# Six slabs kept back ahead of a Strassen pass, and operands moved from GpSimd to VectorE, in a decoder layer

## Chip, core and metric

The kernel runs on one core of a Trainium2 chip. A core has five engines that run side by side, each through its own instructions in order: TensorE (PE in the profile; its weight loads are PEld), VectorE (DVE), ScalarE (ACT), GpSimd (POOL) and SyncE (SP), which here issues most of the DMAs. PE writes its products to PSUM; DVE and ACT work on PSUM and SBUF here, POOL on SBUF. The metric is the time of one execution in microseconds (us).

## The reference, cut to what matters

One decoder layer on 512 tokens of width 2048, in float32:

```
h = RMSNorm(x);  q, k, v for two groups of heads = h @ w_in
A = stick-breaking attention, 16 heads      B = sliding-window attention (128) with sinks, 16 heads
x = x + concat(RMSNorm(A), RMSNorm(B)) @ w_out          # w_out: 2048 x 2048
h = RMSNorm(x);  x = x + (silu(h @ w_gate) * (h @ w_up)) @ w_down     # 5632 wide
out = RMSNorm(x)
```

The change touches the stretch from the sliding-window attention (B) through the output projection `@ w_out` to the first operands of the gate/up product.

## The kernel before

Float32 products are made from rounded halves. Each operand is split into a high half (a copy rounded to the matmul's type, made by ACT) and a low half (the operand less its high half, made by DVE), and high x high, low x high and high x low are added up in PSUM. So each weight that arrives has to be rounded twice before PE can use it, and each left operand too.

**Slabs.** Plain projections run off one list, `queue`, of slabs: a weight tile of 256 rows x 512 columns, read by one DMA on SP's queue into one of three `raw` buffers, rounded by `split` (ACT's `whi` at L221, DVE's `wlo` at L222; two buffers each), then used in eight steps of three matmuls (L382 to L384). `step()` runs one step. At the third step of a slab the two slabs behind it are loaded and the next one is rounded. `pull(ns)` runs steps until a nominal time is used up, `drain(mark)` runs all up to a slab number. `a_end` is the number of slabs up to the end of `outA`, the product with the upper half of w_out (group A's part): four column blocks of four slabs.

**Sliding-window stage.** 18 rounds of a software pipeline over 16 jobs (scores, exponentials, transposes at L1146, products with V at L1159 and L1160), between which `pull(SWFILL / 4, a_end - 3)` runs slabs four times a round. The last job of each head group sums squares of its output into `sqB` (squares by ACT at L729, sums by POOL at L730) and scales the output `oB` by the norm's gain. Behind the rounds three slabs of `outA` are left.

**Strassen pass for group B.** The product of `oB` with the left half of the columns in the lower half of w_out (`OutPass`) is a Strassen-like scheme: seven products in 14 slots (0 to 13), each with weights that are sums or differences of blocks (`sum`, by POOL, from blocks loaded by `load`) and left operands that are sums or differences of blocks of `oB` (`add`) which are rounded (`form`: ACT's high half, then a low half). Plain left operands are rounded by `split_b` into `mhi` and `mlo`. Weights here have their low half taken against a second rounded copy, `hp`, in PSUM. What happens ahead of the pass is a plan by slot numbers: slots -6 to -1, each `b_slot(n)` (loads, sums, roundings of weights for slots n + 1 and n + 2), four steps of the three slabs, then the slot's "late" entries. At slot -4 `sumsq_rstd` turns `sqB` into the norm's factor `rstdB`: matmuls with ones (L735), a copy out of PSUM (L738), a variance `rv` (L278), logarithm and exponential on ACT (L280, L282), and four small DVE operations (L284 to L288).

**Order.** Instructions called through `pV`, `pA`, `pG`, `pT` and `dma` (all at L118 or L100 in the profile) stay in program order on their engine; others may be moved by the scheduler at build time when it thinks an engine free.

**Operands of gate/up.** Behind the pass the right half of the columns follows as eight plain slabs (`add_outB`). Over their steps `h2_split` turns finished columns of x into `xh`, and `form(p, 0, parts)` makes the left operands of another Strassen scheme for the first half of the rows: "+" a sum or difference in place, "h" the high half by ACT, "l" the low half. `form(p, 1, ...)` does so for the second half later.

Of the kernel before, what the change touches and what calls it, by code (L numbers as in the profile page):

```python
# [8 lines left out]
F32 = mybir.dt.float32  # L9
# [3 lines left out]
AF = mybir.ActivationFunctionType  # L13
ALU = mybir.AluOpType
AX = mybir.AxisListType

P = 128
S = 512
NT = S // P
# [3 lines left out]
SBW = 1024  # L23
# [4 lines left out]
EPS = 1e-5  # L28
# [9 lines left out]
def tile_hymba(ctx: ExitStack, tc: tile.TileContext, x, ln_mix, w_in, sb_norm, swa_norm,  # L38
# [6 lines left out]
    const = ctx.enter_context(tc.tile_pool(name="const", bufs=1))  # L45
    sm = ctx.enter_context(tc.tile_pool(name="sm", bufs=4))
# [10 lines left out]
    def open_z(name):  # L57

        if zs[0] is not None:
            zs[0].close()  # L60
        zs[0] = ExitStack()
        zs[1] = zs[0].enter_context(tc.tile_pool(name=name, bufs=1, space=bass.MemoryType.PSUM, reuse_waits="tile"))
# [12 lines left out]
    def pz():  # L75
        return zs[1].tile([P, 512], F32, tag="z", name="z", bufs=4)

    def po():
        return bank("o", 2)
# [22 lines left out]
    def f(ap):  # L102
        return ap.bitcast(F32)

    mm = nc.tensor.matmul
    V = nc.vector
    A = nc.scalar
    G = nc.gpsimd
# [11 lines left out]
    pV, pA, pG, pT = Pinned(V), Pinned(A), Pinned(G), Pinned(nc.tensor)  # L120
# [5 lines left out]
    ones = const.tile([P, P], F32, name="ones")  # L126
# [129 lines left out]
    def pull(ns, mark=None):  # L256

        mark = len(queue) if mark is None else mark
        carry[0] += ns
        while carry[0] > 0 and pos[0] < mark:  # L260
            carry[0] -= step()
# [4 lines left out]
    def drain(mark=None):  # L266

        mark = len(queue) if mark is None else mark
        while pos[0] < mark:
            step()  # L270
# [273 lines left out]
    def at_slot(n, stage, fn, *args):  # L544
        plan.setdefault((n, stage), []).append((fn, args))

    def run(n, stage):
        for fn, args in plan.pop((n, stage), ()):
            fn(*args)
# [182 lines left out]
    def sumsq_rstd(acc, name, pb=None):  # L732
        pb = po() if pb is None else pb
        for t in range(NT):
            mm(pb[:, 2 * t:2 * t + 2], lhsT=acc[:, t * P:(t + 1) * P], rhs=ones[:, 0:2],  # L735
               start=(t == 0), stop=True, skip_group_check=True)
        sst = sm.tile([P, NT], F32, tag="sst", name="sst")
        V.tensor_copy(out=sst, in_=pb[:, 0:2 * NT].rearrange("p (t two) -> p t two", two=2)[:, :, 0])  # L738
        return rstd_from(sst, NT, 1.0 / SBW, name)
# [232 lines left out]
    def at(fn, j):  # L972
        if 0 <= j < NJ:
            fn(*jobs[j])
# [32 lines left out]
    sqB = const.tile([P, S], F32, tag="rbc2", name="sqB")  # L1007
# [73 lines left out]
    a_end = len(queue)  # L1081
# [89 lines left out]
    blks = {}  # L1171
    jobs = [(g, blk) for g in range(4) for blk in range(NT)]
    NJ = len(jobs)
    SWFILL = 5800.0
    pull(2600.0, a_end - 3)
    at(swa_scores, 0)
    stacks = {0: lambda: stack_queries(1, 0), 1: lambda: stack_queries(1, 1), 2: lambda: stack_keys(0, 1),
              5: lambda: stack_keys(1, 0), 6: lambda: stack_keys(1, 1)}
    for j in range(NJ + 2):
        at(swa_exp, j)  # L1180
        if j == 3:
            rstdA = sumsq_rstd(sqA, "rstdA")
        if j in stacks:
            stacks[j]()
        pull(SWFILL / 4, a_end - 3)
        at(swa_tr, j - 1)
        pull(SWFILL / 4, a_end - 3)
        if j == 2:
            drain(swv_end)
        if j + 1 < NJ and jobs[j + 1][1] == 0:  # L1190
            drain(smarks[jobs[j + 1][0]])
        at(swa_av, j - 2)
        pull(SWFILL / 4, a_end - 3)
        at(swa_norm, j)
        at(swa_scores, j + 1)
        pull(SWFILL / 4, a_end - 3)
    drain(a_end - 3)
    kqs.close()

    class OutPass(Block):  # L1200
# [80 lines left out]
    rstd_b = []  # L1281
    open_phase("op", 1, reuse_waits="tile")
    bp = OutPass()
# [5 lines left out]
    for k, q, i in ((-6, "22", 0), (-6, "12", 0), (-5, "11", 0), (-4, "11", 1), (-3, "12", 1), (-2, "22", 1),  # L1289
                    (0, "21", 0), (1, "21", 1)):  # L1290
        at_slot(k, "load", bp.load, q, i)
    for k, fn, *args in ((-5, bp.add, "7", pG), (-4, bp.sum, "7", 0), (-3, bp.sum, "5", 0),
                         (-2, bp.form, "7", pV), (-1, bp.sum, "6", 0), (-1, bp.add, "3", pV),
                         (0, bp.sum, "7", 1), (1, bp.sum, "5", 1), (2, bp.form, "6", pG), (3, bp.sum, "6", 1),
                         (4, bp.sum, "4", 0), (5, bp.sum, "4", 1), (6, bp.form, "5", pG), (8, bp.form, "3", pG)):
        at_slot(k, "sum", fn, *args)
    for k in range(4):
        at_slot(k - 6, "late", split_b, k // 2, k % 2 * 2)
    for k, p in ((-4, "7"), (0, "6"), (4, "5"), (7, "3")):
        at_slot(k, "late", bp.form, p)  # L1300
    at_slot(-3, "late", bp.add, "5", pV)
    at_slot(-2, "late", bp.add, "6", pV)
    for k, p in enumerate(PD):
        at_slot(2 * k + 2, "take", bp.take, p)
    for k, c, h in ((8, 1, 0), (9, 0, 2), (11, 1, 2)):
# [3 lines left out]
    def b_slot(n):  # L1309
        run(n, "load")  # L1310
        run(n, "sum")
        bof(n + 1, "to_hi")
        bof(n + 1, "to_lo")
        bof(n + 2, "to_hp")

    for n in range(-6, 0):
        if n == -4:
            rstd_b.append(sumsq_rstd(sqB, "rstdB", pz()))
        if n == -2:
            open_z("psb")  # L1320
        b_slot(n)
        for _ in range(4):
            step()
        run(n, "late")

# [9 lines left out]
    def e8(name):  # L1335
        return side.tile([P, 4, 512], F32, tag="e8", name=name, bufs=3)
# [28 lines left out]
    def form(p, s, parts="+hl"):  # L1365


        eV, eA = (pV, pA) if s and p not in "17" else (V, A)
        xa, xb = xh[2 * s], xh[2 * s + 1]
        a11, a21 = xa[:, :, 0:256], xa[:, :, 256:512]  # L1370
        if p not in "17":
            a12, a22 = xb[:, :, 0:256], xb[:, :, 256:512]
        if "+" in parts:
            if p == "7":
                src = e8("s3")[:, 0:2, :].rearrange("p u (a b) -> p (u a) b", a=2)
                V.tensor_tensor(out=src, in0=a11, in1=a21, op=ALU.subtract)
            elif p == "5":
                src = a21
                (eV if s else G).tensor_tensor(out=src, in0=a21, in1=a22, op=ALU.add)
            elif p == "6":  # L1380
                src = a11
                (eV if s else G).tensor_tensor(out=src, in0=a21, in1=a11, op=ALU.subtract)
            elif p == "3":
                src = a12
                (pG if s else G).tensor_tensor(out=src, in0=a12, in1=a11, op=ALU.subtract)
            if p not in "124":
                fsrc[p, s] = src
        if p in "124":
            fsrc[p, s] = {"1": lambda: a11, "2": lambda: a12, "4": lambda: a22}[p]()
        src = fsrc[p, s]  # L1390
        if "h" in parts:
            hc[p, s] = form_tile(p, s)
            eA.activation(out=hc[p, s][:, :, 0:256], in_=src, func=AF.Copy)
        if "l" in parts:
            hl = hc[p, s]
            (G if s == 0 and p in "243" else eV).tensor_tensor(out=hl[:, :, 256:512], in0=src, in1=f(hl)[:, :, 0:256],
                                                                op=ALU.subtract)

    def norm_sums(c, t):
        A.activation(out=junk, in_=x2[c][:, t, :], func=AF.Square, accum_out=ss2[:, t, c:c + 1])  # L1400
# [390 lines left out]
    for j in range(NFF):  # L1791
# [7 lines left out]
        late = j < NFF - 1  # L1799
# [31 lines left out]
    for g in range(5):  # L1831
        b0, l = NS + 28 * g, lefts[g]
# [205 lines left out]
```

## Time and profile before

| | us |
|---|---|
| median of 3 runs (2000.39 to 2003.95) | 2000.72 |
| the profiled execution | 2003.73 |
| its span, first to last instruction | 2002.0 |
| PE busy in the span | 1976.7 |
| DVE / ACT / POOL busy | 1511.5 / 1524.3 / 1047.0 |
| mean granted TensorE clock | 0.994 |

The stretch of the change, in the profiled execution: the sliding-window rounds run from about 424 to 580 us, the slots ahead of the pass to 607, the pass to 651, the plain slabs of group B to 707. A timeline row gives start, duration, engine, line of the kernel, operation with tiles out<-in, and in brackets how long the engine was idle before it and what released it. A window's row gives its length and the busy time of PE, PEld, DVE, ACT and POOL, the granted clock, and the share and rate of the DMAs.

### The profile page before, as it was taken

What the parts mean: (1) busy time and instruction counts of PE and PEld (TensorE: products, weight loads), DVE (VectorE), ACT (ScalarE), POOL (GpSimd) and SP (SyncE); (2) the same over time, 40 slices, a digit from 0 to 9 for tenths busy, and PEclk for the clock granted to TensorE, in tenths of its full rate; (3) what the DMA queues carried; (4) which work ended last, traced back from release to release, by engine and by line L of the source; (5) the groups of instructions that cost most, each with busy time, mean ns of one, the idle gap of its engine ahead of it and who ended that gap; (6) DMA issues with size and microseconds to landing.
All of it is one profiled execution on the core that took longest, in us unless ns stands there. A gap on an engine that the chain in (4) does not pass through costs nothing.

```text
span 2002.0 us, 29013 instructions
## 1 busy us (share of the span) xinstructions
PE 1976.7 (99%) x10180; PEld 1688.2 (84%) x10180; DVE 1511.5 (76%) x2066; ACT 1524.3 (76%) x2043; POOL 1047.0 (52%) x458
## 2 busy tenths in 40 slices
PE   9999999999999899999999999999999999999998
PEld 8888888898877788888888888888888888888886
DVE  6676888879878787777777777777777867767767
ACT  6765877868756487777777777777777788788787
POOL 2840000000033376576666657666665778878883
PEclk9999999999998999999999999999999999999999
DMA  6415354422351445445354444535444743433523
GB/s 202 146 53 145 99 136 122 116 80 74 98 188 32 148 121 142 123 115 141 98 141 108 130 124 114 142 98 141 108 129 111 274 147 127 168 126 112 178 79 116
DMA packets 290978, 252.82 MB, mean 126 GB/s; under 512 B 12560, under 2 KB 234832, under 8 KB 288400
## 3 DMA queue, kind: packets, MB, share of 16 engines
q1 hardware_dynamic: 289072, 244.11, 41.8%
q0 software_dynamic: 1376, 5.52, 0.8%
q8 instruction: 81, 1.33, 0.3%
q10 hardware_dynamic: 384, 1.34, 0.2%
q14 instruction: 65, 0.53, 0.1%
HBM read 218.40 MB, written 19.92 MB: 119 GB/s over the span
## 4 chain that ended last, share of the span: by engine, by line
PE 92%; DVE 3%; ACT 2%; issue 2%; POOL 1%; DVEq 0%; ACTq 0%; POOLq 0%
PE o L118 37%; PE m L118 31%; PE m L418 3%; PE m L419 3%; PE m L420 3%; PE z L118 1%; PE z L933 1%; PE m L382 1%; PE m L383 1%; PE m L384 1%; PE o L961 1%; PE o L383 1%; PE o L384 1%; PE o L382 1%; PE z L1146 1%
## 5 line engine op out<-in xcount | busy, mean ns | idle before, releaser
L118 DVE TENSOR_TENSOR wlo<-t,hp 128x1024 fp32r<-128x1024 f32 x253 | 308.4, 1219 | 191.2 <-PE o L118 115.5
L118 POOL TENSOR_TENSOR t<-raw,t 128x1024 f32<-128x1024 f32 x111 | 282.6, 2546 | 281.0 <-ACT hp L118 268.7
L118 ACT ACTIVATE whi<-t 128x1024 fp32r<-128x1024 f32 x253 | 268.5, 1061 | 130.0 <-PE o L118 78.3
L118 POOL TENSOR_TENSOR t<-raw,raw 128x1024 f32<-128x1024 f32 x118 | 305.9, 2596 | 29.4 <-issue 11.7
L118 PE MATMUL o<-hca,whi 128*128 128x512 f32 x880 | 307.5, 391 | 0.0
L118 DVE TENSOR_TENSOR wlo<-raw,hp 128x1024 fp32r<-128x1024 f32 x191 | 233.2, 1221 | 92.9 <-issue 51.6
L118 ACT ACTIVATE whi<-raw 128x1024 fp32r<-128x1024 f32 (+1 forms) x193 | 204.1, 1058 | 107.4 <-PE m L118 75.2
L118 ACT ACTIVATE hp<-t 128x1024 fp32r<-128x1024 f32 x253 | 255.2, 1009 | 8.0 <-POOL t L118 4.3
L118 PE MATMUL o<-hca,wlo 128*128 128x256 f32 x880 | 244.0, 280 | 0.0
L118 ACT ACTIVATE hp<-raw 128x1024 fp32r<-128x1024 f32 x195 | 196.7, 1009 | 3.1 <-DMA raw<-in_w_down_dram 1.9
L118 PEld LDWEIGHTS o<-hca,whi 128*128 128x128 f32 x880 | 164.2, 187 | 35.8
L118 PE MATMUL m<-hca,whi 128*128 128x512 f32 x528 | 186.3, 392 | 1.1 <-DVE hca L118 1.1
L118 PEld LDWEIGHTS o<-hca,wlo 128*128 128x128 f32 x880 | 165.6, 189 | 0.4
L730 POOL TENSOR_TENSOR sqA<-sqA,oc 128x512 f32<-128x512 f32 x7 | 10.1, 1437 | 273.9 <-ACT oc L729 273.9
L118 PE MATMUL m<-whi,dca 128*128 128x512 f32 x592 | 146.9, 389 | 0.0
L118 PE MATMUL o<-whi,dca 128*128 128x512 f32 x592 | 146.8, 389 | 0.0
L118 PE MATMUL m<-hca,wlo 128*128 128x256 f32 x528 | 146.3, 280 | 0.0
L118 PEld LDWEIGHTS o<-whi,dca 128*128 128x128 f32 x592 | 111.1, 188 | 23.0
L118 PEld LDWEIGHTS m<-whi,dca 128*128 128x128 f32 x592 | 111.1, 188 | 23.0
L222 DVE TENSOR_TENSOR wlo<-raw,whi 128x1024 fp32r<-128x1024 f32 x79 | 100.2, 1268 | 35.6 <-ACT whi L221 34.1
L118 PE MATMUL m<-hcs,whi 128*128 128x512 f32 x352 | 125.9, 392 | 0.0
L418 PE MATMUL m<-hhi,whi 128*128 128x512 f32 x320 | 125.8, 393 | 0.0
(391 smaller groups left out, 5204.5 us busy)
## 6 DMA issues: line engine op xcount, KB each, us to landing
raw<-in_w_gate_up_dram SPq DMA_DIRECT2D x348, 256.0 KB, 5.2
raw<-in_w_down_dram SPq DMA_DIRECT2D x68, 512.0 KB, 5.0
raw<-in_w_in_dram SPq DMA_DIRECT2D x35, 512.0 KB, 4.7
raw<-in_w_in_dram SPq DMA_DIRECT2D x66, 256.0 KB, 4.0
raw<-in_w_out_dram SPq DMA_DIRECT2D x28, 512.0 KB, 3.8
aT<-w SPq DMA_DIRECT2D x44, 256.0 KB, 3.5
xd<-aT SPq DMA_DIRECT2D x10, 1024.0 KB, 6.6
rx<-in_w_down_dram SPq DMA_DIRECT2D x20, 512.0 KB, 5.6
```

What stands on the lines that cost most here:

```text
L118: return lambda *a, **k: tc.keep_in_program_order(fn(*a, **k))
L222: V.tensor_tensor(out=lo, in0=raw, in1=f(hi), op=ALU.subtract)
L382: mm(o, lhsT=lh[:, sl], rhs=hi[:, j, :], start=first, stop=False, skip_group_check=halves)
L383: mm(o, lhsT=lh[:, sl], rhs=lo[:, j, :], start=False, stop=False, skip_group_check=halves)
L384: mm(o, lhsT=ll[:, sl], rhs=hi[:, j, :], start=False, stop=(k == nslab * a - 1), skip_group_check=halves)
L418: mm(o, lhsT=wh, rhs=xh, start=(k == 0), stop=False)
L419: mm(o, lhsT=wh, rhs=xl, start=False, stop=False)
L420: mm(o, lhsT=wl, rhs=xh, start=False, stop=(k == KT - 1))
L730: G.tensor_tensor(out=acc, in0=acc, in1=t, op=ALU.add)
L933: mm(zb[:, o:o + r.shape[1]], lhsT=lhsT, rhs=r, start=False, stop=last, skip_group_check=True)
L961: mm(H.ob[:, c0:S], lhsT=vb, rhs=r[:, o:o + S - c0], start=(k == 3 and r is B.h), stop=(k == 0 and r is B.l), skip_group_check=True)
L1146: nc.tensor.transpose(out=pb[:, hh * P:(hh + 1) * P], in_=B.s[hh // 2][:, hh % 2, j * P:(j + 1) * P], identity=ident)
```

## The change

- Six slabs of `outA` are kept for the slots ahead of the pass, not three; `SWFILL` is 5200, not 5800; the slots run from -8 to -1 with six steps each, not from -6 with four.
- The roundings by `split_b` and the difference for the seventh product move to slots -8 and -7, the sums on `oB` and the seventh product's low half to -6 and -5. POOL's weight sums and the loads keep their slots (-6 to 1).
- `sumsq_rstd` is taken apart: matmuls and variance at -8 (the variance read from PSUM, without the copy), logarithm and exponential at -6, the small operations at -5.
- For the first half of the gate/up operands, the three sums and the three low halves that POOL made are made by DVE.

```diff
-    SWFILL = 5800.0
-    pull(2600.0, a_end - 3)
+    SWFILL = 5200.0
+    pull(2600.0, a_end - 6)
...
-        pull(SWFILL / 4, a_end - 3)
+        pull(SWFILL / 4, a_end - 6)
...
-    drain(a_end - 3)
+    drain(a_end - 6)
...
-    for k, fn, *args in ((-5, bp.add, "7", pG), (-4, bp.sum, "7", 0), (-3, bp.sum, "5", 0),
-                         (-2, bp.form, "7", pV), (-1, bp.sum, "6", 0), (-1, bp.add, "3", pV),
-                         (0, bp.sum, "7", 1), (1, bp.sum, "5", 1), (2, bp.form, "6", pG), (3, bp.sum, "6", 1),
-                         (4, bp.sum, "4", 0), (5, bp.sum, "4", 1), (6, bp.form, "5", pG), (8, bp.form, "3", pG)):
+    for k, fn, *args in ((-4, bp.sum, "7", 0), (-3, bp.sum, "5", 0), (-1, bp.sum, "6", 0), (0, bp.sum, "7", 1),
+                         (1, bp.sum, "5", 1), (2, bp.form, "6", pG), (3, bp.sum, "6", 1), (4, bp.sum, "4", 0),
+                         (5, bp.sum, "4", 1), (6, bp.form, "5", pG), (8, bp.form, "3", pG)):
         at_slot(k, "sum", fn, *args)
-    for k in range(4):
-        at_slot(k - 6, "late", split_b, k // 2, k % 2 * 2)
-    for k, p in ((-4, "7"), (0, "6"), (4, "5"), (7, "3")):
-        at_slot(k, "late", bp.form, p)
-    at_slot(-3, "late", bp.add, "5", pV)
-    at_slot(-2, "late", bp.add, "6", pV)
+    rB = {}
+    def rstdb_sum():
+        pb = pz()
+        for t in range(NT):
+            mm(pb[:, 2 * t:2 * t + 2], lhsT=sqB[:, t * P:(t + 1) * P], rhs=ones[:, 0:2], ...)
+        rB["v"] = sm.tile([P, NT], F32, tag="rv", name="rv")
+        pV.tensor_scalar(out=rB["v"], in0=pb[...], scalar1=1.0 / SBW, scalar2=EPS, op0=ALU.mult, op1=ALU.add)
+    def rstdb_exp():
...
+        pA.activation(out=l, in_=rB["v"], func=AF.Ln)
...
+        pA.activation(out=rB["r"], in_=l, func=AF.Exp, scale=-0.5)
+    def rstdb_make():
...
+        pV.tensor_tensor(out=rstd_b[0], in0=r, in1=t, op=ALU.mult)
+    for k, fn, *args in ((-8, bp.add, "7", pG), (-8, rstdb_sum), (-8, split_b, 0, 0), (-8, split_b, 0, 2),
+                         (-7, split_b, 1, 0), (-7, split_b, 1, 2), (-7, bp.form, "7"), (-6, rstdb_exp),
+                         (-6, bp.add, "5", pV), (-6, bp.add, "6", pV), (-5, rstdb_make), (-5, bp.form, "7", pV),
+                         (-5, bp.add, "3", pV), (0, bp.form, "6"), (4, bp.form, "5"), (7, bp.form, "3")):
+        at_slot(k, "late", fn, *args)
...
-    for n in range(-6, 0):
-        if n == -4:
-            rstd_b.append(sumsq_rstd(sqB, "rstdB", pz()))
+    for n in range(-8, 0):
...
-        for _ in range(4):
+        for _ in range(6):
             step()
...
-                (eV if s else G).tensor_tensor(out=src, in0=a21, in1=a22, op=ALU.add)
+                eV.tensor_tensor(out=src, in0=a21, in1=a22, op=ALU.add)
...
-                (eV if s else G).tensor_tensor(out=src, in0=a21, in1=a11, op=ALU.subtract)
+                eV.tensor_tensor(out=src, in0=a21, in1=a11, op=ALU.subtract)
...
-                (pG if s else G).tensor_tensor(out=src, in0=a12, in1=a11, op=ALU.subtract)
+                (pG if s else V).tensor_tensor(out=src, in0=a12, in1=a11, op=ALU.subtract)
...
-            (G if s == 0 and p in "243" else eV).tensor_tensor(out=hl[:, :, 256:512], in0=src, in1=f(hl)[:, :, 0:256],
-                                                                op=ALU.subtract)
+            eV.tensor_tensor(out=hl[:, :, 256:512], in0=src, in1=f(hl)[:, :, 0:256], op=ALU.subtract)
```

More of the change, by code (lines that the diff above doesn't have):

```diff
@@ L1184, in tile_hymba @@
             stacks[j]()
-        pull(SWFILL / 4, a_end - 3)
+        pull(SWFILL / 4, a_end - 6)
         at(swa_tr, j - 1)
-        pull(SWFILL / 4, a_end - 3)
+        pull(SWFILL / 4, a_end - 6)
         if j == 2:
@@ L1192, in tile_hymba @@
         at(swa_av, j - 2)
-        pull(SWFILL / 4, a_end - 3)
+        pull(SWFILL / 4, a_end - 6)
         at(swa_norm, j)
         at(swa_scores, j + 1)
-        pull(SWFILL / 4, a_end - 3)
-    drain(a_end - 3)
+        pull(SWFILL / 4, a_end - 6)
+    drain(a_end - 6)
     kqs.close()
@@ L1296, in tile_hymba @@
         at_slot(k, "sum", fn, *args)
-    for k in range(4):
-        at_slot(k - 6, "late", split_b, k // 2, k % 2 * 2)
-    for k, p in ((-4, "7"), (0, "6"), (4, "5"), (7, "3")):
-        at_slot(k, "late", bp.form, p)
-    at_slot(-3, "late", bp.add, "5", pV)
-    at_slot(-2, "late", bp.add, "6", pV)
+    rB = {}
+    def rstdb_sum():
+        pb = pz()
+        for t in range(NT):
+            mm(pb[:, 2 * t:2 * t + 2], lhsT=sqB[:, t * P:(t + 1) * P], rhs=ones[:, 0:2],
+               start=(t == 0), stop=True, skip_group_check=True)
+        rB["v"] = sm.tile([P, NT], F32, tag="rv", name="rv")
+        pV.tensor_scalar(out=rB["v"], in0=pb[:, 0:2 * NT].rearrange("p (t two) -> p t two", two=2)[:, :, 0],
+                         scalar1=1.0 / SBW, scalar2=EPS, op0=ALU.mult, op1=ALU.add)
@@ new lines, in rstdb_exp @@
+    def rstdb_exp():
+        l = sm.tile([P, NT], F32, tag="rl", name="rl")
+        pA.activation(out=l, in_=rB["v"], func=AF.Ln)
+        rB["r"] = sm.tile([P, NT], F32, tag="rr", name="rr")
+        pA.activation(out=rB["r"], in_=l, func=AF.Exp, scale=-0.5)
+    def rstdb_make():
+        r, t = rB["r"], sm.tile([P, NT], F32, tag="rt", name="rt")
+        pV.tensor_tensor(out=t, in0=r, in1=r, op=ALU.mult)
+        pV.tensor_tensor(out=t, in0=t, in1=rB["v"], op=ALU.mult)
+        pV.tensor_scalar(out=t, in0=t, scalar1=-0.5, scalar2=1.5, op0=ALU.mult, op1=ALU.add)
+        rstd_b.append(const.tile([P, NT], F32, name="rstdB"))
+        pV.tensor_tensor(out=rstd_b[0], in0=r, in1=t, op=ALU.mult)
```

## The prediction

> **What bounds the kernel now.** I read the page first, then the list of what PE waited for, then the order in time around the longest of those waits, on PE, POOL and DVE in turn. Rows of a timeline are start, duration, engine, line, operation, and in brackets the idle time before it and who ended it; rows of the wait list are total us, times, longest.
>
> ```profile
> span 2002.0 us, 29013 instructions
> PE 1976.7 (99%) x10180; PEld 1688.2 (84%) x10180; DVE 1511.5 (76%) x2066; ACT 1524.3 (76%) x2043; POOL 1047.0 (52%) x458
> ```
> ```profile
> PE m L383 <- DVE wlo L222: 6.8, 2, 4.6
> PE m L118 <- DVE wlo L118: 2.9, 1, 2.9
> PE m L382 <- ACT whi L221: 2.1, 1, 2.1
> ```
>
> PE has work for 1976.7 of 2002.0 us, so an edit off PE can win 25 us at most, plus what matmuls lose on a slow clock. Of the idle time 11.8 us is in these three rows, and all three mean the low or the high half of a weight slab. They stand in two places, both of which the diff edits. The first is just ahead of the Strassen pass of the output projection:
>
> ```profile
> 579.40 0.40 PE L1160 MATMUL z<-plo,swv 128*128 128x512 f32 x1
> ...
> 593.91 0.39 PE L384 MATMUL o<-whi,mlo 128*128 128x512 f32 x1
> 596.35 0.50 PE L382 MATMUL m<-whi,mhi 128*128 128x512 f32 x1 [2.05 <-ACT whi L221]
> 599.10 0.80 PE L383 MATMUL m<-wlo,mhi 128*128 128x512 f32 x1 [2.25 <-DVE wlo L222]
> ```
> ```profile
> 611.71 2.07 PE L118 MATMUL m<-wlo,mhi 128*128 128x512 f32 x4 [2.87 <-DVE wlo L118]
> 613.58 1.91 PE L118 MATMUL m<-whi,mhi 128*128 128x512 f32 x4
> ...
> 618.35 2.01 PE L118 MATMUL o<-whi,vf 128*128 128x512 f32 x8
> ```
>
> From 613.58 on four matmuls take 1.91 us where eight take 2.01 at 618.35: behind such idle time the clock is halved for some us. What the place costs in all: the slab that ends at 593.91 + 0.23 = 594.14 is followed by one more slab and the first product, 24 matmuls each. A slab without a wait is 24 x 0.23 = 5.5 us, so the next product could start at 605.1. It starts at 618.35. **The first place costs 13.3 us**: 7.2 idle, 6.1 slow clock.
>
> Why the halves are late, from POOL and DVE in the same stretch:
>
> ```profile
> 582.12 2.66 POOL L730 TENSOR_TENSOR sqB<-sqB,oc 128x512 f32<-128x512 f32 x2 [1.48 <-ACT oc L729]
> 584.73 0.79 POOL L118 DMA_DIRECT2D x<-in_x_dram  x1
> 585.54 2.65 POOL L118 TENSOR_TENSOR t<-oB 128x1024 f32<-128x1024 f32 x1
> 588.15 3.37 POOL L118 TENSOR_TENSOR t<-raw,raw 128x1024 f32<-128x1024 f32 x1
> 591.60 3.25 POOL L118 TENSOR_TENSOR raw<-raw,rx 128x1024 f32<-128x1024 f32 x1
> 594.93 2.36 POOL L118 TENSOR_TENSOR t<-raw,raw 128x1024 f32<-128x1024 f32 x1
> 603.72 2.39 POOL L118 TENSOR_TENSOR t<-raw,raw 128x1024 f32<-128x1024 f32 x1 [6.43 <-DVE vf L118]
> ```
> ```profile
> 585.85 6.75 DVE L118 TENSOR_TENSOR mlo<-oB,mhi 128x1024 fp32r<-128x1024 f32 x2
> ...
> 592.71 2.16 DVE L278 TENSOR_SCALAR rv<-sst 128x4 f32<-128x4 f32 x1
> ...
> 597.82 1.23 DVE L222 TENSOR_TENSOR wlo<-raw,whi 128x1024 fp32r<-128x1024 f32 x1
> ...
> 603.51 1.45 DVE L1074 SCALAR_TENSOR_TENSOR x<-m,rstdA,x 128x512 f32<-128x512 f32 x2
> ```
>
> While POOL works, two roundings take 6.75 us, and a 128x4 operation takes 2.16, both ending as a POOL operation ends; with POOL idle a rounding is 1.23. The two engines alternate: one POOL operation of 2.4, one DVE operation of 1.1. The two operations at 603.51 read a PSUM bank and take 0.73 each although POOL starts at 603.72: those aren't held. The Trainium skill (SBUF — State Buffer, "Who interferes with whom") says that a VectorE instruction with two SBUF inputs and a GpSimd instruction that reads SBUF exclude each other, the later one blocking for the whole instruction. By that rule 6.75 would be one POOL operation waited for at each rounding, and the trace agrees.
>
> The second place is the first half's operands of the gate/up stage:
>
> ```profile
> 671.74 3.32 POOL L1396 TENSOR_TENSOR hca<-xh,hca 128x1024 fp32r<-128x1024 f32 x1
> ```
> ```profile
> 662.47 1.22 DVE L222 TENSOR_TENSOR wlo<-raw,whi 128x1024 fp32r<-128x1024 f32 x1
> 667.07 5.79 DVE L1396 TENSOR_TENSOR hca<-xh,hca 128x1024 fp32r<-128x1024 f32 x2 [3.38 <-ACT hca L1393]
> 672.78 3.35 DVE L222 TENSOR_TENSOR wlo<-raw,whi 128x1024 fp32r<-128x1024 f32 x1
> ```
> ```profile
> 671.20 0.39 PE L382 MATMUL m<-whi,mhi 128*128 128x512 f32 x1
> 676.19 0.80 PE L383 MATMUL m<-wlo,mhi 128*128 128x512 f32 x1 [4.60 <-DVE wlo L222]
> ...
> 682.79 0.39 PE L384 MATMUL o<-whi,mlo 128*128 128x512 f32 x1
> ```
>
> That slab runs from 671.20 to 683.02, 11.8 us in place of 5.5: **the second place costs 6.3 us**. The cause is the same: POOL and DVE exclude each other.
>
> **The change, part by part.** Everything is PE time; the matmuls are the same, only their order moves.
>
> *Filler of the sliding-window stage.* Six slabs are held back, so 15.5 us less filler for 18 rounds; SWFILL falls by 0.6 in nominal ns, 0.63 us on PE. What a round then lacks is cover for DVE:
>
> ```profile
> 449.98:513.50 63.52, 63.17 (x329) 52.59 (x327) 62.08 (x156) 51.47 (x125) 2.38 (x2) 1.00 0.24 75
> 513.50:557.04 43.54, 43.54 (x228) 36.65 (x227) 37.35 (x91) 33.34 (x88) 5.91 (x5) 1.00 0.31 97
> ```
>
> The columns are length, then busy PE, PE load, DVE, ACT, POOL. In the first seven of these twelve rounds DVE is busy 62.1 of 63.5 us. Filler brings DVE work too (a slab's 1.2 us rounding and about as much around it per 5.5 us), so a round loses 0.63 us of PE and 0.27 of DVE. Seven rounds: PE 59.1, DVE 60.2, and DVE's 1.4 us of idle time were waits. So 1.1 to 2.5 us of new PE waits in many small pieces; bounds 0 (DVE catches up) and 4.4 (7 x 0.63). I take **+2.0**, nearest to both sums. The later five rounds have 6 us of slack on DVE: nothing. The 15.5 held back exceed the 18 x 0.6 = 10.8 that the pulls give up, so the last 4.7 us of pulls find the queue empty; before, the four steps behind 579.40 were such filler. They stood where the second row shows cover to spare: nothing.
>
> *Sum of squares.* Its matmuls now stand six steps (4.1 us) behind the last product, not eight and the filler that was left. The squares are ready at 582.12 + 2.66 = 584.78, 5.0 us behind that product's end (579.80). PE, in order, waits **+1.2** (bounds 0 and 1.3: nothing on POOL ahead of the two adds is new). The variance reads PSUM now, so the 2.16 of the old row should go; one copy of 0.15 goes with it. Exp and the four small operations come later, behind roundings, and nobody waits for them.
>
> *Roundings and POOL's sums.* In the slots the sums stay at -4, -3 and -1, behind the roundings at -8 and -7. But POOL isn't bound by PE's steps; it starts a sum when its operands are there. Those come over SP's queue (a row of its waits, and the loads' row of the DMA view, whose last number is us to landing):
>
> ```profile
> SPq L100 <- PE z L1160: 8.2, 1, 8.2
> raw<-in_w_out_dram SPq DMA_DIRECT2D x8, 512.0 KB, 3.7
> ```
>
> SP waited for the last product's release of memory, not for a slot; a load lands 3.7 us later. The slab loads that are now ahead of it need buffers that are free by then, except one that a rounding near the last product's end frees. So I expect the operands 4 to 7.5 us behind the last product, and POOL again without a pause from its difference of oB on. Counting from the end of the last product: squares 5.0; difference on POOL 5.3 to 7.95; variance 6.6. Now DVE and POOL alternate: rounding 9.0, sum 11.4, rounding 12.5, sum 14.9, low half of the third slab 16.0, sum 18.4, two roundings 20.6, takes from PSUM 22.7, the two adds 25, low half of the fourth slab 26.2. PE needs the third at 13.4 and the fourth at 18.9 (1.2 included). Its 26.2 is 7.3 late: **+7.3**, in two pieces of 2.6 and 2 to 4.7, and a half clock behind, for which the second place's 6.3 less 4.6 gives 1.7: **+1.7**. Bounds: 0, if the sums come behind the roundings, and 13.3, the old loss. I take the schedule, since the rows at 585.85 are the same operations side by side. After that DVE has only 5 operations ahead of the pass, and the low halves of the last slabs and of the first product come in time: the old 13.3 is gone. **First place: -13.3 + 1.2 + 7.3 + 1.7 = -3.1.**
>
> The buffer that the pass takes leaves two for the slabs; a load then waits for a rounding, and rounding to rounding is a landing of 3.7 and two roundings of 1.2, 6.1 us, over two slabs of 5.5 each: covered. The residual's load on POOL (0.79, at 584.73) moves with its slab behind the first sum, beside DVE's next rounding. ACT's high halves read oB and aren't held by POOL; they run ahead of DVE's.
>
> *Later operands by DVE.* Six POOL operations (three sums, three low halves) become six of 1.22 on DVE, 7.3 us; three DVE operations lose their holding (5.79 and 3.35 become 2.4 and 1.2: 5.5 less). DVE is free from 663.7, and the chain 5, 6, low half, then the slab's own low half (ready once ACT is no longer held in front of it by POOL's sums) ends near 668.5, needed at 671.4. **-6.3** (bounds -6.3, all that is lost there, and 0, if the slab's low half is queued last).
>
> **Sum:** 2.0 - 3.1 - 6.3 = -7.4. The profiled execution took 2003.73 us (span 2002.0), 3.0 above the median of the three runs, 2000.72; I take the difference off the median: 1993.3, say 1993.
>
> **Rivals.** *A: the cover works.* If POOL's sums really come behind (operands land after 11 us), the third and fourth low halves are in time: 9.0 us more, 1984. For it: a landing can take longer than 3.7 when other loads are in the queue. Against: 585.54 to 594.93 leaves no gap on POOL.
>
> *B: no gain ahead of the pass and part lost in the rounds.* Late halves cost the old 13.3 again and the rounds 4.4, or the second place keeps its wait: 2000.72 - 6.3 + 4.4 = 1998.8, no difference that can be told (0.2%, or 4 us, is about what a measurement of this kernel can tell). For it: DVE is what both places want more of.
>
> *C: slower, by the clock.* The sliding-window waits gather into single ones. Behind 2.87 us of idle time the rows show the half clock; where DVE's lag becomes one wait of that length each second round, four such at 1.7 us and 4.4 idle add 11.2 in place of 2.0; with the first place as under B: 2000.72 + 11.2 - 6.3 = 2005.6. It decides from about 13 us lost in the rounds or 10 with no gain ahead of the pass. Against it: the wait would be spread, since every round needs DVE. The Trainium skill (TensorE: Matmul & The Clock Gate, "What's actually happening") puts the halving behind an idle window of about 3.4 us; the trace shows it behind 2.87 after a thin stretch, so waits of 0.6 should not do it by either.
>
> **How the numbers follow.** The sum as worked out 0.47, with its own range 1989 to 1997; A 0.24; B 0.19; C 0.10. Faster by over 0.2% (under 1996.7): nearly all of the first and A, 0.69. Same: B and the edge of the first, 0.21. Slower: 0.10. The range 1983 to 2000 holds A, the sum and most of B.
>
> **What would show it.** Right: no L1379, L1382, L1385 or L1396 on POOL and no PE wait over 1 us in the second place; PE waiting about 1.2 us for its matmuls on the squares; POOL's difference and three sums within 15 us of the last product with roundings of 3.4 us between; a PE wait of 2 to 5 us for L222's low half three or four slabs ahead of the pass and none at its start; small waits of PE for DVE's probabilities in the rounds. Wrong: POOL's sums behind the roundings (then A), or a half clock inside the rounds (then C).

## The result, and the profile after

| | before | after |
|---|---|---|
| median of four runs, us | 2000.71 (2000.39 to 2003.95) | 1991.14 (1989.09 to 1992.18) |
| the profiled execution, us | 2003.73 | 1990.91 |
| its span, us | 2002.0 | 1989.2 |
| PE busy, us | 1976.7 | 1972.2 |

The changed kernel is faster by half a per cent: 0.9947 of the time before, 95% interval 0.993 to 0.9965. The forecast was 1993.0. The runs of one kernel scatter (the kernel before from 2000.39 to 2004.48 us over all groups), so times are compared by medians, and a row of a profile is that of one execution. The page of the kernel after, its span and its busy times:

```profile
span 1989.2 us, 29012 instructions
...
PE 1972.2 (99%) x10180; PEld 1685.0 (85%) x10180; DVE 1503.0 (76%) x2071; ACT 1524.6 (77%) x2043; POOL 1027.6 (52%) x452
```

The head of its list of PE's waits (total us, times, longest). Of the three rows of before that the prediction started from two are gone and the first is down from 6.8 to 0.7. Two are new: on x (L1074, the "takes": VectorE adds a finished column block from PSUM to x, which frees the PSUM bank) and on sqB:

```profile
PE o L382 <- DVE x L1074: 2.3, 1, 2.3
PE z L1301 <- POOL sqB L730: 1.4, 1, 1.4
PE o L118 <- POOL ones L127: 1.2, 1, 1.2
PE m L118 <- DVE hca L118: 1.1, 1, 1.1
PE m L383 <- DVE wlo L222: 0.7, 1, 0.7
```

PE's timeline of the kernel after, from the squares' matmuls to the first product with `vf` in the pass (start, duration, operation, idle time before it):

```profile
571.47 1.05 PE L1301 MATMUL z<-ones,sqB 128*128 128x2 f32 x8 [1.37 <-POOL sqB L730]
...
575.08 0.63 PE L382 MATMUL m<-whi,mhi 128*128 128x512 f32 x1
...
581.54 0.50 PE L383 MATMUL m<-wlo,mhi 128*128 128x512 f32 x1 [0.74 <-DVE wlo L222]
...
586.67 0.79 PE L382 MATMUL o<-whi,mhi 128*128 128x512 f32 x1 [2.30 <-DVE x L1074]
587.27 0.63 PE L383 MATMUL o<-wlo,mhi 128*128 128x512 f32 x1
...
612.83 1.98 PE L118 MATMUL o<-whi,vf 128*128 128x512 f32 x8
```

The row `o<-whi,vf` is a ruler for all that follows. Ahead of it lies everything that the first part of the change can move, and behind it nothing differs between the kernels whose later operands are made by DVE: from its start to the end of the span there are 1376.4 us in each of them (here 1989.2 - 612.83). Before, it started at 618.35, with 1383.65 behind it. So the span's 12.8 us split into **5.5 ahead of the row (first part) and 7.3 behind it (second part)**.

How much the first place still loses is seen by laying it beside a kernel of the experiments that has no PE wait there (`e8_both_later`). A window's row: length, then busy PE, PE load, DVE, ACT, POOL, then the clock. First after, then that kernel:

```profile
565.40:612.83 47.43, 43.02 (x177) 34.45 (x176) 31.68 (x31) 20.37 (x26) 22.36 (x11) 0.93 0.52 167
```
```profile
565.38:604.36 38.98, 38.98 (x177) 32.44 (x176) 28.40 (x31) 20.73 (x26) 22.21 (x11) 1.00 0.59 203
```

The same 177 matmuls take 47.43 us and 38.98. Of the 8.45 lost, 4.41 is idle time (1.37 + 0.74 + 2.30, the three brackets above) and 4.04 is longer matmul time (43.02 - 38.98). Most of that is half clock, in two bouts of eight matmuls, one behind the squares (572.95 to 576.34) and one behind the wait for x (586.67 to 590.12): they follow each other after about 0.43 us, not 0.23, and lose 1.6 us a bout, 3.2 together. The rest lies around the waits, mostly the ends of the matmuls in front of them, which count as busy.

POOL and DVE of the kernel after in that stretch:

```profile
571.37 2.36 POOL L118 TENSOR_TENSOR t<-oB 128x1024 f32<-128x1024 f32 x1
574.47 2.60 POOL L118 TENSOR_TENSOR t<-raw,raw 128x1024 f32<-128x1024 f32 x1 [0.74 <-DMA raw<-in_w_out_dram]
...
577.80 2.60 POOL L118 TENSOR_TENSOR raw<-raw,rx 128x1024 f32<-128x1024 f32 x1
580.48 3.26 POOL L118 TENSOR_TENSOR t<-raw,raw 128x1024 f32<-128x1024 f32 x1
```
```profile
572.56 0.16 DVE L118 TENSOR_SCALAR rv<-z 128x4 f32<-128x4 f32 x1 [4.81 <-PE z L1301]
572.64 5.51 DVE L118 TENSOR_TENSOR mlo<-oB,mhi 128x1024 fp32r<-128x1024 f32 x2
578.07 1.40 DVE L1074 SCALAR_TENSOR_TENSOR x<-m,rstdA,x 128x512 f32<-128x512 f32 x2
579.39 2.10 DVE L222 TENSOR_TENSOR wlo<-raw,whi 128x1024 fp32r<-128x1024 f32 x1
581.41 4.55 DVE L118 TENSOR_TENSOR mlo<-oB,mhi 128x1024 fp32r<-128x1024 f32 x2
585.88 1.40 DVE L1074 SCALAR_TENSOR_TENSOR x<-o,rstdA,x 128x512 f32<-128x512 f32 x2
...
588.33 1.21 DVE L222 TENSOR_TENSOR wlo<-raw,whi 128x1024 fp32r<-128x1024 f32 x1
```

POOL's four operations run from 571.4 to 583.7, right beside the four roundings of oB, as before. The second pair of roundings is held until 585.9, and the two takes of finished columns stand behind it in DVE's order. PE waits for the PSUM banks that these takes empty: that is the 2.30.

In the second place POOL has no row left, and PE no wait between 640 and 700 us. DVE's rows there, none of them held (the last is three operations):

```profile
657.99 1.22 DVE L1400 TENSOR_TENSOR xh<-xh 128x1024 f32<-128x1024 f32 x1
...
661.50 1.23 DVE L222 TENSOR_TENSOR wlo<-raw,whi 128x1024 fp32r<-128x1024 f32 x1
...
663.77 3.49 DVE L1417 TENSOR_TENSOR hca<-xh,hca 128x1024 fp32r<-128x1024 f32 x3
```

### The profile page after: what moved, and what is told of

Its sections match the earlier page's. It is cut to its first block, busy times and chain, and to the rows that moved or that the text cites. A ratio compares the mean times of both kernels' runs of the same rounds, so it can differ in the third digit from the quotient of the medians.

```text
span 1989.2 us, 29012 instructions
## 1 busy us (share of the span) xinstructions
PE 1972.2 (99%) x10180; PEld 1685.0 (85%) x10180; DVE 1503.0 (76%) x2071; ACT 1524.6 (77%) x2043; POOL 1027.6 (52%) x452
## 4 chain that ended last, share of the span: by engine, by line
PE 97%; DVE 1%; ACT 1%; DMA 0%; issue 0%; POOL 0%; DVEq 0%; SPq 0%; ACTq 0%; POOLq 0%
PE o L118 37%; PE m L118 31%; PE m L418 4%; PE m L419 4%; PE m L420 4%; PE z L118 1%; PE m L383 1%; PE m L382 1%; PE m L384 1%; PE z L933 1%; PE o L382 1%; PE o L961 1%; PE o L383 1%; PE o L384 1%; PE z L1146 1%; PE z L886 1%
## 5 line engine op out<-in xcount | busy, mean ns | idle before, releaser
L221 ACT ACTIVATE whi<-raw 128x1024 fp32r<-128x1024 f32 x79 | 83.4, 1056 | 68.0 <-PE o L384 28.1
```

Source lines behind the costliest of these rows:

```text
L221: A.activation(out=hi, in_=raw, func=AF.Copy)
```

## The experiments

All share the ruler. "Slabs" are the slabs kept for the slots, "order" is that of the roundings, squares and sums on oB in the slots. The first column of numbers is the median over the runs, then the ratio to the kernel before, which ran beside it (its medians there: 2002.5 to 2003.5), then the start of the ruler row in the profile.

| kernel | slabs | order | further | us | ratio, 95% | ruler |
|---|---|---|---|---|---|---|
| e2_dve_forms | 3 | old | second part of the change alone | 1995.69 | 0.9965 (0.9953 to 0.9978) | 618.38 |
| e4_three_slabs | 3 | new | | 1992.63 | 0.9952 (0.9939 to 0.9964) | 614.22 |
| e9_old_order | 6 | old | | 1984.3 | 0.991 (0.9895 to 0.9925) | 606.20 |
| the changed kernel | 6 | new | | 1991.14 | 0.9947 (0.993 to 0.9965) | 612.83 |
| e1_pool_forms | 6 | new | second part undone | 1998.16 | 0.9978 (0.9969 to 0.9987) | 613.40 |
| e3_loads_late | 6 | new | three loads later | 1988.23 | 0.9932 (0.992 to 0.9945) | 610.20 |
| e5_sums_later | 6 | new | squares' matmuls later | 1988.33 | 0.9929 (0.9917 to 0.9942) | 610.05 |
| e7_both | 6 | new | e3 and e5 | 1983.8 | 0.991 (0.9897 to 0.9924) | 605.36 |
| e8_both_later | 6 | new | e5, all six loads later still | 1982.45 | 0.9902 (0.9887 to 0.9917) | 604.36 |
| e12_spread | 6 | new | one rounding a slot | 1988.3 | 0.9928 (0.9914 to 0.9942) | 611.89 |
| e6_fill4400 | 6 | new | SWFILL 4400 | 1992.37 | 0.995 (0.9936 to 0.9963) | 614.20 |
| e10_both_three | 3 | new | e3 and e5 | 1992.71 | 0.9952 (0.9939 to 0.9964) | 615.64 |
| e11_old_late | 3 | old | three loads later | 1995.3 | 0.9965 (0.9953 to 0.9978) | 617.17 |

**The two parts one by one.** `e1_pool_forms` is the changed kernel with POOL making the later operands again:

```diff
-                eV.tensor_tensor(out=src, in0=a21, in1=a22, op=ALU.add)
+                (eV if s else G).tensor_tensor(out=src, in0=a21, in1=a22, op=ALU.add)
... (the other two sums alike)
-            eV.tensor_tensor(out=hl[:, :, 256:512], ...)
+            (G if s == 0 and p in "243" else eV).tensor_tensor(out=hl[:, :, 256:512], ...)
```

> The changed kernel, with the first half's later operands back on POOL (three sums, three low halves); the six slabs stay. If DVE's freedom from POOL is what the second part brings, the wait of 4.6 us for a slab's low half (L222) comes back in the plain slabs of group B, with its half clock: some 6.3 us more than the changed kernel, 1997.5. Rival: the wait was an echo of the first place (the slabs come in late there), then it stays away and the time stays near 1991.

`e2_dve_forms` is the kernel before with the reverse of these lines.

> The kernel before, with only the second part of the change (later operands by DVE). If the two parts are independent: 2000.7 - 6.3 = 1994.4, the first place as before (three long waits of PE ahead of the pass), no PE wait for a low half in the plain slabs. Rival: the parts need each other, then 1998 or more.

Both came out as the theory had it. The waits of PE in `e1_pool_forms`, whose first row is the second place, back at its old size:

```profile
PE m L383 <- DVE wlo L222: 4.5, 1, 4.5
PE o L382 <- DVE x L1074: 4.5, 1, 4.5
```

(The wait for x is 4.5 in this profile and 2.3 in that of the changed kernel; the ruler is 0.6 us later.) The second part is worth 0.35% (7.0 us) alone and the first 0.22% (4.4 us) alone; together that would be 0.57%, and the changed kernel has 0.53%, so no effect of one part on the other is seen. The rulers agree: with the second part alone the row stands at 618.38, as before (618.35), and with the first alone there are 1384.1 us behind it, as before (1383.65).

**What in the first place still costs.** `e3_loads_late` lets POOL's operands arrive later:

```diff
-    for k, q, i in ((-6, "22", 0), (-6, "12", 0), (-5, "11", 0), (-4, "11", 1), ...
+    for k, q, i in ((-4, "22", 0), (-4, "12", 0), (-4, "11", 0), (-4, "11", 1), ...
```

> The changed kernel, with the loads of the first blocks for POOL's sums at slot -4, not -6 and -5: on SP's queue they then stand behind a slab load that waits for the third slab's low half, so the sums really come behind the first roundings. My theory (alternating with POOL holds DVE back): the third slab's low half and the takes behind two roundings are in time; the waits of 0.74 and 2.3 us and the half clock of about 1.4 us behind them go: about -4.4, 1986.7. The wait for the squares (1.4 us and its half clock) stays. Rival: DVE is late because it stands behind the variance, which waits for the squares, and POOL matters little: 1990 to 1991.

POOL's first weight sum starts at 586.65 in place of 574.47. The first pair of roundings is held for only about 1 us, beside POOL's difference of oB (571.50 to 573.86), and the second not at all; one wait of PE stands later:

```profile
572.77 3.31 DVE L118 TENSOR_TENSOR mlo<-oB,mhi 128x1024 fp32r<-128x1024 f32 x2
...
579.84 2.36 DVE L118 TENSOR_TENSOR mlo<-oB,mhi 128x1024 fp32r<-128x1024 f32 x2
```
```profile
593.49 0.50 PE L383 MATMUL m<-wlo,mhi 128*128 128x512 f32 x1 [1.66 <-DVE wlo L222]
```

The wait for x is gone. What is left is the wait for the squares with its half clock, and this one of 1.66 us for a later slab's low half, which is new. The ruler moved by 2.6 us. The time, 1988.2, lies between the theory's 1986.7 and the rival's 1990.

`e5_sums_later` takes the squares' matmuls, and the variance with them, from ahead of the roundings to behind them (the variance stands in DVE's order, so a late square also held the roundings):

```diff
-    ... (-8, bp.add, "7", pG), (-8, rstdb_sum), (-8, split_b, 0, 0), (-8, split_b, 0, 2),
-        (-7, split_b, 1, 0), (-7, split_b, 1, 2), (-7, bp.form, "7"), (-6, rstdb_exp),
+    ... (-8, bp.add, "7", pG), (-8, split_b, 0, 0), (-8, split_b, 0, 2),
+        (-7, split_b, 1, 0), (-7, split_b, 1, 2), (-7, rstdb_sum), (-7, bp.form, "7"), (-6, rstdb_exp),
```

> The changed kernel, with the matmuls on the squares and the variance behind the four roundings (slot -7, not ahead of them in -8). PE's wait for the squares (1.4 us) and the half clock behind it (1.6) go in any case: 3.0. Under the rival of the run with late loads (DVE stands behind the variance) the roundings start 5 us earlier and the other waits go as well: 7.4 less, 1983.7. Under my theory they start earlier but meet POOL's sums all the same: 3 to 5 less, 1986 to 1988.

PE's waits in the place are down to one, behind which the clock is halved for over 3 us:

```profile
PE o L382 <- DVE x L1074: 3.2, 1, 3.2
```

The ruler moved by 2.8 us: the squares' wait with its bout (3.0) and the 0.74 are gone, and the wait for x has grown from 2.30 to 3.19. The time, 1988.3, is just above the theory's 1986 to 1988 and far from the rival's 1983.7. The first pair of roundings now starts at 568.34, ahead of POOL's sums, and the second at 576.31 still falls among them (6.72 us for the two).

`e7_both` has both edits, and `e8_both_later` the second one with all six loads and the first two sums at slot -2.

> Late loads (slot -4) and the squares' matmuls behind the four roundings together. The variance no longer holds DVE, and the first roundings end before POOL's sums begin: no PE wait for the squares, none for the takes. What can be left is the wait for the fourth slab's low half against the sums (1.7 us with late loads alone; the sums now start with the third slab's low half, some 3 us earlier): 1985 to 1987. If the two gains just added up (3.7 and 3.6 less than the changed kernel): 1984.

> As the run with both, with all six loads for the first sums at slot -2: on SP's queue behind the last slab's load, so POOL's sums begin only behind the fourth slab's low half. By my theory no PE wait over 1 us is left ahead of the pass: 1983 to 1984. Rival: the sums are now late for the pass itself (the second product's weights at slot 2), and a PE wait for a low half or for ACT's copies appears in the pass: 1986 or more.

With both edits the ruler is 7.5 us earlier than in the changed kernel, more than 2.6 and 2.8 together: `e3_loads_late` had left the wait for the squares, `e5_sums_later` the one for x, and each is what the other takes away. (Expected were 1985 to 1987, or 1984 if the gains just added up; it took 1983.8.) `e8_both_later` has no PE wait left in the place at all, nor in the pass, where the rival had looked for one, and it is the fastest of all the kernels: 0.9902 of the time before, 8.5 us under the changed kernel by the ruler. What is left in front of its row is matmuls on full clock (the 38.98 of 38.98 above).

**Was it the six slabs or the order?** `e4_three_slabs` keeps everything of the change but the slabs:

```diff
-    SWFILL = 5200.0
+    SWFILL = 5800.0
-    drain(a_end - 6)
+    drain(a_end - 3)
...
-        for _ in range(6):
+        for _ in range(3):
```

> The changed kernel with the old cover: three slabs kept, SWFILL 5800, three steps a slot in the eight slots; the new order of the roundings and the second part stay. If the slabs are what helps the first place (DVE's some 25 us of work behind the last product, with POOL's turns, needs 33 us of PE beside it), its loss goes back to about the old 13 us: some 5 us more than the changed kernel, 1996 to 1997. Rival: the order helps, not the cover: 1991 to 1992.

Our expectation was 4 us too high; the rival, 1991 to 1992, was nearly right about this kernel's time (1992.6). Its waits, and DVE's row of the four roundings:

```profile
PE m L383 <- DVE wlo L222: 6.5, 1, 6.5
```
```profile
585.50 13.25 DVE L118 TENSOR_TENSOR mlo<-oB,mhi 128x1024 fp32r<-128x1024 f32 x4
```

Four roundings held by POOL, one after the other, 13.25 us, and a low half behind them: one wait of 6.5 us. By the ruler it loses only 1.4 us more than six slabs did with three waits and two bouts of half clock. From this alone we expected the cover by itself to be worth as little as the order by itself. So we tried the other half, `e9_old_order`: six slabs and six steps a slot, but the order of the kernel before.

```diff
-    for k, fn, *args in ((-8, bp.add, "7", pG), (-8, rstdb_sum), (-8, split_b, 0, 0), (-8, split_b, 0, 2),
-                         (-7, split_b, 1, 0), (-7, split_b, 1, 2), ...
+    for k in range(4):
+        at_slot(k - 6, "late", split_b, k // 2, k % 2 * 2)
+    ... (add "7" at -5, form "7" at -4 and -2, adds "5", "6", "3" at -3, -2, -1, as before)
     for n in range(-8, 0):
+        if n == -4:
+            rstd_b.append(sumsq_rstd(sqB, "rstdB", pz()))
```

> The changed kernel with six slabs kept and six steps a slot, but the order of the kernel before in the slots (roundings of oB at slots -6 to -3, squares' matmuls at -4, the difference of the seventh product at -5), and DVE making the later operands. It is the cover without the order. The kernel with three slabs and the new order lost as much ahead of the pass as the changed kernel (the pass's row o<-whi,vf at 614.22 against 612.83, and 604.36 in the kernel with nothing lost). Theory: cover alone is worth as little as order alone, because POOL's sums come at the same time after the last product (about 9 us) and meet the roundings, which now begin 8 us later: the pass's row at 613 to 616, a time of 1992 to 1995 where the changed kernel has 1992. Rival: with the six slabs there is time enough for everything in whatever order, the row at 605 to 608, 1984 to 1987.

The expectation fell again, and the rival's 1984 to 1987 holds: 1984.3. Ahead of the row PE waits once, 1.22 us:

```profile
602.43 1.19 PE L118 MATMUL m<-wlo,mhi 128*128 128x512 f32 x4 [1.22 <-DVE wlo L118]
...
606.20 1.98 PE L118 MATMUL o<-whi,vf 128*128 128x512 f32 x8
```

And it isn't that POOL came later. POOL and DVE of `e9_old_order`:

```profile
576.00 2.42 POOL L118 TENSOR_TENSOR t<-raw,raw 128x1024 f32<-128x1024 f32 x1 [2.12 <-DVE wlo L222]
...
579.17 2.58 POOL L118 TENSOR_TENSOR raw<-raw,rx 128x1024 f32<-128x1024 f32 x1
581.83 3.26 POOL L118 TENSOR_TENSOR t<-raw,raw 128x1024 f32<-128x1024 f32 x1
```
```profile
574.73 1.22 DVE L222 TENSOR_TENSOR wlo<-raw,whi 128x1024 fp32r<-128x1024 f32 x1
...
577.45 2.05 DVE L118 TENSOR_TENSOR mlo<-oB,mhi 128x1024 fp32r<-128x1024 f32 x1
579.42 3.41 DVE L222 TENSOR_TENSOR wlo<-raw,whi 128x1024 fp32r<-128x1024 f32 x1
582.76 3.41 DVE L118 TENSOR_TENSOR mlo<-oB,mhi 128x1024 fp32r<-128x1024 f32 x1
```

POOL's sums stand 1.5 us later than in the changed kernel and hold DVE nearly as long: three operations take 8.87 us where 3 x 1.22 would be 3.66, 5.2 us of holding; in the changed kernel five took 5.51 + 2.10 + 4.55 = 12.16, where 6.1 would do, 6.1 us of holding. But here a slab's takes and its low half (574.73) are through before the first rounding, and one rounding a slot lies between two low halves. PE doesn't see this holding. Its one wait of 1.22 us comes later: two sums on oB are held beside POOL's next sums (1.88 us at 596.03 and 2.75 at 598.49), and the low half of the pass's first weights stands behind them.

So the two halves of the first part work against each other. By the ruler, the old order gains 12.2 us from the six slabs (618.38 to 606.20); the new order gains 1.4 from them (614.22 to 612.83). With three slabs the new order gains 4.2; with six it loses 6.6. The medians give the same picture: 11.4 and 1.5 for the slabs, 3.1 gained and 6.8 lost for the order.

**What in the new order is at fault.** `e12_spread` moves only the roundings of the changed kernel, to one a slot:

```diff
-    ... (-8, split_b, 0, 0), (-8, split_b, 0, 2), (-7, split_b, 1, 0), (-7, split_b, 1, 2), ...
+    ... (-8, split_b, 0, 0), (-7, split_b, 0, 2), (-6, split_b, 1, 0), (-5, split_b, 1, 2), ...
```

> The changed kernel with one thing moved: the four roundings of oB, two each in slots -8 and -7, stand one each in slots -8, -7, -6 and -5. The squares' matmuls, the loads and POOL's sums stay where the change put them. With six slabs and the old order, which has one rounding a slot, the pass's row o<-whi,vf stood at 606.20, with six slabs and the new order at 612.83. Theory: the pairs are the fault. A rounding held by POOL delays whatever stands behind it on VectorE; behind a pair stand a slab's two takes from PSUM and its low half, so PE waits 0.7 and 2.3 us there and then runs on half clock; one a slot, each hold is made good within a slot. What is left is the wait for the squares and the half clock behind it, 3 us: the row at 607.5 to 609, a time of 1986 to 1988. Rival: it is the early squares' matmuls and the other moved operations, and the holds only move: the row at 611 to 613, 1990 to 1992.

The ruler says 611.89, inside the rival's 611 to 613; the median, 1988.3, lies just above the theory's 1986 to 1988. The two disagree because the profile is of an execution of 1990.04 us: two of the five runs took 1990.0 to 1990.1, the other three 1987.8 to 1988.3. PE's waits in the profile:

```profile
PE m L383 <- DVE wlo L222: 2.0, 2, 1.1
...
PE o L382 <- DVE x L1074: 1.2, 1, 1.2
PE z L1301 <- POOL sqB L730: 1.2, 1, 1.2
```

The wait of 2.3 is cut to 1.2, under what halves the clock, but two for low halves took its place. Pairs are worth 0.9 us by the profiles and 2.8 by the medians, part of the 6.6 but not all. On PE's side the 6.6 is accounted for: from the last product to the ruler the changed kernel loses 8.45 us to its three waits and two bouts, the old order 1.5 to its one wait (and its last product ends 0.3 us later). Which difference in order removes which wait is open: moving the squares' matmuls was worth 2.8 by itself (`e5_sums_later`) and later loads 2.6 (`e3_loads_late`), but these don't add up simply, as `e7_both` showed, and no kernel with spread roundings and late squares was run.

**Later loads without the slabs.** Do the loads alone do it? `e10_both_three` is `e7_both` with three slabs (the edit of `e4_three_slabs`), and `e11_old_late` is `e2_dve_forms` with the loads of `e3_loads_late`.

> The kernel with the three loads at slot -4 and the squares' matmuls behind the roundings (1983.8), but with three slabs kept, SWFILL 5800 and three steps a slot. Theory: what costs is that POOL's sums hold DVE's roundings; in the kernel with three slabs and the early loads four roundings took 13.25 us instead of 4.7, and PE waited 6.5 us; with the loads twelve steps (8.2 us) later the roundings run alone and most of that wait is gone: the row o<-whi,vf at 605 to 609, a time of 1984 to 1988. Rival: DVE and POOL have about 25 us of work ahead of the pass, and three slabs give 16.4 us of matmuls; the wait stays or moves to the pass's first weights: the row at 611 to 616, 1990 to 1995.

> The kernel before with DVE making the later operands (1995.7) and, alone, the three loads of the pass moved from slots -6, -6 and -5 to -4, eight steps (5.5 us) later; three slabs, old order. Theory: the loads that run ahead are the fault, not the order or the cover; the pair of roundings that took 6.75 us beside POOL's sums runs alone, and half or more of the 14 us lost ahead of the pass goes: the row o<-whi,vf at 608 to 613 in place of 618.4, a time of 1985 to 1990. Rival: the later roundings (slots -4 and -3) then meet the sums instead, or the pass's first weights come late: 1993 to 1997.

Both theories fell, and both rivals held. With 24 steps in place of 48, PE waits 7.0 us in the first (four roundings take 11.19 us from 586.52 on, and POOL's sums begin at 589.20, in the midst of them: four slots of three steps, 8.2 us, were too short to keep them apart), and 4.8, 2.7 and 1.5 in the second, two of these inside or at the start of the pass:

```profile
PE m L118 <- DVE wlo L118: 4.8, 1, 4.8
PE m L118 <- DVE x L1074: 2.7, 1, 2.7
PE m L383 <- DVE wlo L222: 1.5, 1, 1.5
```

Three slabs are too little matmul for DVE's and POOL's work in either order. The cover was needed after all.

**How much filler the rounds can give up.** `e6_fill4400` has SWFILL 4400 in place of 5200.

> The changed kernel with SWFILL 4400: 0.84 us of PE less in each sliding-window round, 0.36 us of DVE less with it; the filler is then run behind the rounds, so PE's work is the same. The changed kernel has no PE wait in the rounds although DVE is busy 60.0 of 62 us. By the prediction's rule (what a round lacks of DVE time, PE waits) seven rounds lose 7 x 0.48 less the 2 us that DVE has left: 1.4 us or more of PE waits for DVE's operands, up to 6. Rival: the build's order puts other filler there and the rounds still hide it: none. In both the filler behind the rounds lets the squares come in time, so PE's wait for them (1.4 us and a half clock) goes: 1988 under the rival, 1990 to 1994 by the rule.

The last product comes 4.3 us earlier (560.86 against 565.17), more slabs then stand between it and the slots, and the squares no longer wait. But the rounds now show seven small waits of PE, 4.4 us together, the longest 1.19, in windows where DVE is busy throughout:

```profile
500.00:512.00 12.00, 11.34 (x61) 9.09 (x60) 11.91 (x29) 9.24 (x24) 3.44 (x3) 1.00 0.33 91
...
524.00:536.00 12.00, 10.57 (x59) 8.93 (x60) 11.92 (x31) 7.14 (x19) 0.00 (x0) 1.00 0.32 89
```

At 5200 nothing is lost in the rounds; at 4400 4.4 us are, and the later stretch gains only 3: the ruler is 1.4 us later, as the expectation's rule had it (1990 to 1994; 1992.4).

## Why the prediction was right or wrong

It had the sign, the places and the engines right, and the sum too small: 7.4 us against 9.6 by the medians, 12.8 by the profiles, and 10.6 by the ratio (0.53% of the 2002.5 that the kernel before takes in most runs). The first runs were low for that kernel (four later groups of 9 to 15 runs have medians of 2002.5 to 2003.5), so the medians understate the gain, and taking the sum off 2000.72 hid about 2 us of the shortfall in the time forecast. That the time came so near is thus partly luck, and so is the sum of the terms: the filler and the low halves were put 6.3 us too high together, the half clock 2.3 too low. Of the signs named beforehand, the wait for the squares and the empty second place came; the wait of 2 to 5 us for a low half and the small waits in the rounds did not. By terms:

**Filler, +2.0: wrong, 0.** Two windows that cover most of the rounds in the kernel after:

```profile
449.00:511.00 62.00, 62.00 (x327) 51.77 (x325) 59.95 (x155) 52.46 (x130) 2.07 (x2) 1.00 0.23 71
511.00:555.00 44.00, 44.00 (x234) 36.87 (x233) 40.29 (x105) 35.39 (x91) 7.14 (x6) 1.00 0.37 117
```

PE is busy all of both. The lower of the two bounds was right. The step took DVE for the bound of these rounds, with 60.2 us of work for PE's 59.1; the first row has DVE busy 59.95 of 62.0 us, 96.7%, no more than the 97.7% of before (62.08 of 63.52). So there was slack that the step didn't count; where in a round it lies wasn't looked at. The term begins only between 5200 and 4400, as `e6_fill4400` shows.

**Squares, +1.2: right, 1.37,** with a consequence that wasn't seen: behind this wait and eight matmuls of 128x2 the clock is halved for over 3 us, which loses 1.6 more, so the wait costs about 3.0 in all.

**Low halves, +7.3: half right.** POOL's difference and sums came where the schedule put them (571.4 to 583.7 is 5.8 to 18.2 us behind the last product's end at 565.57; forecast: 5.3 to 18.4), though the first sum waited for its load, 8.9 us behind, where the forecast had the operands at 4 to 7.5. The roundings are held beside them, and the third slab's low half was late (0.74, forecast 2.6). It ended 15.9 us behind, as scheduled (16.0), but PE asked for it at 15.2 and not at 13.4: the half clock behind the squares wasn't in the due times. The fourth slab's wasn't late at all: it ended at 24.0 and was asked for at 25.7. The schedule ended at "takes from PSUM 22.7, two adds 25, low half 26.2" and looked only for low halves; it passed over the takes, which PE needs sooner, since they free the bank that the next column block is added up in. They ended at 587.3, 21.7 us behind, 1 us ahead of the forecast, and PE waited 2.30 for them. In all 3.0 us, in place of 7.3. (One reading behind the schedule was off, without harm to it: the pair of 6.75 us ends at 592.60, 1.1 us behind a POOL operation, not with it.)

**Half clock, +1.7: right for a bout, too small in all, 4.0:** two bouts of 1.6 in place of one, and what lies around three waits.

**First place: -3.1 forecast, -5.5 measured by the ruler,** the rounds included, where the forecast was -1.1 with them.

**Second place, -6.3: right, -7.3.** The one wait of 4.6 and its half clock are the 6.3; the kernel before also had a wait of 0.63 for a bank behind them, which the forecast left standing. `e2_dve_forms` measures it alone: 0.35%, 7 us.

Of the rivals, A (the cover works, 1984) wasn't the changed kernel, in which POOL's sums came among the roundings, as the argument against A had it. But the six slabs with the old order reach A's time, 1984.3 (`e9_old_order`), and not for A's reason: POOL's sums stand among the roundings in that kernel too. B and C have nothing for them: no wait in the rounds, and the pass's first weights in time.

What the prediction never asked is whether the new order was better than the old one under the same cover. It costed the roundings' new place by when they'd end and not by what they'd stand in front of. The Trainium skill (SBUF — State Buffer, "Who interferes with whom") fits the pairs held here, as the prediction said: two roundings take 2.36 us with POOL idle and 4.55 to 6.75 among its sums. How long they are held was thus foreseen; what stands behind them was not, and the order as a whole was worth 6.6 us.

## What to carry to other kernels

When an engine is held up by another for some microseconds, look in its program order at what stands behind the held operation and when that is due: in the old order the takes that free PSUM banks and the next weights' low half stand ahead, and the bulk work one piece a slot between them, and with six slabs that order was 6.6 us better (spreading the bulk work alone gave 0.9 to 2.8 of it). Test a change of two halves as a two by two: one half without the other looked worthless here from one side (1.4 us) and was worth 12.2 from the other. Once there is cover, moving the loads that start the interfering engine, and the matmul that waits, is cheap: two edits of a line or two each took another 7.5 us off, and with three slabs the same edits gave nothing (1992.71 against 1992.63).

## What the runs showed of the hardware

- The clock. A wait of 1.66 us (`e3_loads_late`) or 1.61 (`e6_fill4400`) ahead of a matmul left it at full speed; waits of 2.30 and of 3.19 (`e5_sums_later`) halved it for over 3 us. 1.37 and 1.15 us (`e12_spread`) halved it too when eight 128x2 matmuls of 1.05 us in all followed, and those matmuls behind 0.28 us (`e4_three_slabs`) didn't. So these thin matmuls acted like idle time, and in these runs the idle time that halves the clock lies between 1.7 and 2.3 us, less than the window of about 3.4 that the Trainium skill (TensorE: Matmul & The Clock Gate, "What's actually happening") gives.
- The VectorE operations that read PSUM here weren't held: the variance took 0.16 us at 572.56 with POOL at work, and 2.16 in the kernel before, where it read SBUF; two takes took 1.40 us at 578.07, also beside POOL.
